# Moving the weight sums of two seven-product down projections to an earlier stage and another engine

## Chip, core and metric

The kernel runs on one core of a Trainium2 chip. The metric is the device time of one execution in microseconds, the median of several runs.

## What is computed

Two transformer blocks in sequence on one sequence of 1024 tokens with 1024 features, all in float32. What the change touches are both feed-forward networks, the first block's gated unit and its attention:

```python
# first block
xn = rms_norm(x, mix_norm_g)
q, k, v, f_logit, z = split(xn @ w_in)
attn = forgetting_attention(q, k, v, log_sigmoid(f_logit + b_f))   # 8 heads, causal
sgu  = spatial_gating(gelu(z), ...)
x = x + concat(rms_norm(attn), rms_norm(sgu)) @ w_out
gate, up = split(rms_norm(x) @ w_gate_up)
x = rms_norm(x + (silu(gate) * up) @ w_down, final)                 # w_down: 2816 x 1024
# second block: convolutions, a delta rule in chunks, stick-breaking attention, w_mix_out
u = causal_dwconv(rms_norm(x) @ w_ffn_up); gate, val = split(u)
x = x + (silu(gate) * val) @ w_ffn_down                             # w_ffn_down: 2816 x 1024
```

## The kernel before

**Products.** A float32 matrix product is done as three passes of a reduced type: each operand is cut into a high part (a cast on ScalarE, `split`, L256) and a low part (a subtraction on VectorE, L257), and `mm3` issues high x high, high x low and low x high. The order of the instructions on each engine is made by a scheduler at build time from priorities that follow the program's order; at run time every engine works through its own list in order and waits on semaphores. A tile is followed by the regions that are read and written.

**Stages of block 1.** `zphase` projects `z` in four column blocks (b = 0 to 3, eight token tiles t each) and does the gated unit. `attention` then takes four pairs of heads p = 0 to 3: `gemm(p + 1)` makes q, k and v of the next pair while `attend(p)` does the scores, the exponentials, the transposes and the products with v of this one. The output of pair p goes to `OT[:, p, :]` (16 KB per partition in all): ScalarE copies one half of the sum out of PSUM (L657) and VectorE adds the other (L658). The bank `O` that it comes from has one buffer. The pool engine (GpSimd) has two memsets (`ql`, L527) between the start-up and the loads of `x` behind the attention (L743).

**Down projection.** `ffn` computes the hidden values in units and spills them to memory (`hd`). Then `strassen` multiplies the first 20 of 22 blocks of 128 hidden features as a 2 x 2 partition with seven products (`DOWN`, in the order A11 B11, A12 B21, S3 T3, A22 T4, S1 T1, S2 T2, S4 B22), each of ND = 10 steps k; a step is four token tiles of three passes, 12 matmuls of 128 x 512. A are the hidden values, B the weights (quarters of 1280 x 512, 2.6 MB each), S and T their sums:

S3 = A11 - A21, S1 = A21 + A22, S2 = A22 - S3, S4 = A12 - S2; T3 = B22 - B12, T1 = B12 - B11, T2 = B22 - T1, T4 = B21 - T2.

- *The A side.* `operand(i)` makes the sums for step i and cuts A or S into a slot of a ring `ah`; it runs AR = 3 steps ahead of the matmuls. `DE` says which engine does which sum. A22 comes through two slots `a22`, loaded step by step (`load22`, L1218).
- *The B side.* The pool `W` (class `Weights`) gives each weight piece a slot: a load through a ring of two raw buffers on the SP queue, a cut into one of three high/low buffers, in a fixed order. `add_down` makes the slots of the down projection, one for two steps k. B11, B12 and B21 lie whole in SBUF, loaded by `fetch` at the start of the stage (with A11, A12 and A21); B22 comes through the ring, once for T3 and once for its own product. When the slot of T3 is cut, VectorE makes T3 and T1, and the pool engine T2; when that of T4 is cut, the pool engine makes T4 (L845).

The matmuls' sums in PSUM are added into `x` by VectorE at L980 (`add`), two per step (`PB`), after a product has ended.

Of the kernel before, what the change touches and what calls it, by code (L numbers as in the profile page):

```python
# [40 lines left out]
ND, AR, A2, PB = 10, 3, 2, 2  # L41
# [11 lines left out]
DE = dict(S3=pool_, T3=vec_, T1=vec_, T2=pool_, T4=pool_, S1=vec_, S2=vec_, S4=pool_)  # L53
# [104 lines left out]
class Kern:  # L158
# [6 lines left out]
    def setup(self):  # L165
        tc, nc = self.tc, self.nc
        self.const = c = tc.alloc_tile_pool(name="const", bufs=1)
        self.xnp = tc.alloc_tile_pool(name="xn", bufs=1)
        self.W = Weights(self, tc.alloc_tile_pool(name="w", bufs=1), 2, 3)
        self.dram = tc.alloc_tile_pool(name="dram", bufs=1, space=DRAM)  # L170
        self.hd = self.dram.tile([NF, P, S], F32, name="hd")
        self.ident = c.tile([P, P], F32, name="ident")
        make_identity(nc, self.ident)
        self.eps = c.tile([P, 1], F32, name="eps")
        nc.vector.memset(self.eps, EPS)
# [175 lines left out]
    def block1(self):  # L351
# [22 lines left out]
        self.zphase(mid, zb, zu, fl)  # L374
# [6 lines left out]
    def zphase(self, mid, zb, zu, fl):  # L381
# [80 lines left out]
        zl = z2.tile([P, NT, 512], F32R, name="zl")  # L462
        for t in range(NT):
            zmm(1, t)
            st = z2.tile([P, 6], F32, tag="bst", name="bst", bufs=2)
# [3 lines left out]
        for t in range(NT):  # L469
            zmm(2, t)  # L470
            y = z2.tile([P, 512], F32, tag="lny", name="lny", bufs=2)
# [5 lines left out]
        for t in range(NT):  # L477
            zmm(3, t)

# [12 lines left out]
        pool.release()  # L492

# [25 lines left out]
    def attention(self, mid, qkv, zu, cT, fl, OT, wo):  # L519
# [6 lines left out]
        for x in range(2):  # L526
            nc.gpsimd.memset(ql[x][64 * (1 - x):64 * (2 - x)].bitcast(F32), 0.0)  # L527
# [288 lines left out]
    def plan_ffn(self, which):  # L816
# [13 lines left out]
        for _, name in DOWN:  # L830
            if which == 1 and name == "T2":
                rest()
            for k in range(0, ND, 2):
                slots[name, k] = self.add_down(home, name, k, dn)
# [4 lines left out]
    def add_down(self, home, name, k, dn):  # L839

        W, nc = self.W, self.nc
        raw = W.load([(0, dn[:, ND + k:ND + k + 2, 512:])], 2, 512) if name in ("T3", "B22") else None

        def tt(out, in0, in1, what):
            DE[what](nc).tensor_tensor(out=out, in0=in0, in1=in1, op=ALU.subtract)  # L845

        def make(hi, lo):
            out = []
            for j in range(2):
                h, l = (v[:, j * 512:(j + 1) * 512] for v in (hi, lo))  # L850
                b11, b12, b21 = (home.get((q, k + j)) for q in ("B11", "B12", "B21"))
                b22 = None if raw is None else W.raw[raw][:, j * 512:(j + 1) * 512]
                if name == "T3":
                    src = home["T3", j]
                    tt(src, b22, b12, "T3")
                    tt(b12, b12, b11, "T1")
                    tt(b11, b22, b12, "T2")
                else:
                    src = dict(B11=b11, B21=b21, T4=b21, T1=b12, T2=b11, B22=b22)[name]
                    if name == "T4":  # L860
                        tt(b21, b21, b11, "T4")
                self.split(h, l, src)
                out.append((h, l))
            return out
        return W.slot(make, raw)
# [76 lines left out]
    def ffn(self, which):  # L942
# [193 lines left out]
        def fetch(q, k0, k1):  # L1136

            f = k0 + ND * ((q[2] if q[0] == "A" else q[1]) == "2")
            c = 512 * ((q[1] if q[0] == "A" else q[2]) == "2")
            src = self.hd[f:f + k1 - k0, :, c:c + 512].rearrange("k p c -> p k c") if q[0] == "A" else \  # L1140
                dn[:, f:f + k1 - k0, c:c + 512]
# [9 lines left out]
        def down_load():  # L1151

            for q, part in (("A11", "hi0"), ("B11", "lo0")):
                place(q, self.xnp.tile([P, KT, 512], F32, tag=part, name=q), 0, KT)
            for k in range(0, KT, 2):
                fetch("A11", k, k + 2)
                fetch("B11", k, k + 2)
# [3 lines left out]
        def down_open():  # L1161
# [4 lines left out]
            ring["ah"] = [d.tile([P, 2, 512], F32R, name=f"ah{i}") for i in range(AR)]  # L1166
            d = tc.alloc_tile_pool(name=f"dm{which}", bufs=1, reuse_waits="tile")
            dp.append(d)
            for j in range(2):
                home["T3", j] = d.tile([P, 512], F32, name=f"T3{j}")  # L1170
            ring["a22"] = [d.tile([P, 512], F32, name=f"a22{i}") for i in range(A2)]
            for q in ("A11", "B11", "A21", "B12"):
                place(q, d.tile([P, ND - KT, 512], F32, name=f"{q}x"), KT, ND)
            for q, part in (("A21", "hi1"), ("B12", "lo1")):
                place(q, self.xnp.tile([P, KT, 512], F32, tag=part, name=q), 0, KT)
            fetch("A11", KT, ND)
            fetch("B11", KT, ND)
            fetch("A12", 0, ND // 2)
            fetch("A12", ND // 2, ND)
            for i in range(AR):  # L1180
# [39 lines left out]
        def load_rest():  # L1220

            dp.pop().release()
# [8 lines left out]
        def strassen():  # L1231
            pool.release()
            last = None
            d2 = tc.alloc_tile_pool(name=f"dr{which}", bufs=1, side="right", reuse_waits="tile")
            dp.append(d2)
            self.psum(dn=(1, 8))
            place("B21", d2.tile([P, ND, 512], F32, name="B21"), 0, ND)
            for q in ("B21", "A21", "B12"):
                cuts = ((0, ND // 2), (ND // 2, ND)) if q == "B21" else ((0, KT // 2), (KT // 2, KT), (KT, ND))
                for k0, k1 in cuts:  # L1240
                    fetch(q, k0, k1)
            for k in range(A2):
                load22(k)
            sums = []
            for i, (name, bname, k) in enumerate(steps):
# [14 lines left out]
                w = W.get(slots[bname, k - k % 2])[k % 2]  # L1260
# [20 lines left out]
            if which == 1:  # L1281
                W.done(slots[DOWN[-1][1], ND - 2])
            return last
# [13 lines left out]
        else:  # L1297
# [3 lines left out]
            dp[1].release()  # L1301
# [956 lines left out]
```

## Time and profile before

| | |
|---|---|
| median of 3 runs (lowest to highest) | 2526.09 us (2524.6 to 2533.17) |
| the profiled execution: time, span | 2535.99 us, 2534.3 us |
| TensorE busy, granted clock | 2425.8 us (96%), 0.984 |
| VectorE, ScalarE, GpSimd busy | 1849.4, 1148.9, 431.7 us |
| first block's `z` projections; attention | about 17 to 118 us; 118 to 425 us |
| down projections in seven products | from 949 us and from 2288 us |

The span runs from the first to the last instruction. Engine names in the profile: PE is TensorE (PEld its weight loads), DVE VectorE, ACT ScalarE, POOL GpSimd, SP the queue from which most transfers are issued. A granted clock of 1.00 is the upper of TensorE's two levels (2.4 GHz), a mean below it says that part of the time was spent at the lower one (1.2 GHz).

### The profile page before, as it was taken

How to read it: one execution, taken by the hardware profiler on the slowest of the kernel's cores; microseconds unless marked ns; L12 is line 12 of the kernel's file. 1: busy time of each engine (PE TensorE's matmuls, PEld its weight loads, DVE VectorE, ACT ScalarE, POOL GpSimd, SP SyncE). 2: the span in 40 equal slices, each digit the busy share in tenths (PEclk: the TensorE clock that was granted, in tenths of full speed). 3: DMA queues.
4: the chain of work that ended last, by engine and by line, in shares of the span. 5: the costliest groups of instructions: out<-in, count | busy, mean ns of one | idle time of the engine just before them, and what ended most of it. 6: DMA issues, size and time to landing. Idle time of an engine off the chain costs nothing. (4 is left out here: it accounts for less than half of the span.)

```text
span 2534.3 us, 33313 instructions
## 1 busy us (share of the span) xinstructions
PE 2425.8 (96%) x12360; PEld 1997.5 (79%) x12360; DVE 1849.4 (73%) x3346; ACT 1148.9 (45%) x2298; POOL 431.7 (17%) x402
## 2 busy tenths in 40 slices
PE   7999999999999999899999999989889999999898
PEld 7977779978888887588877777879678888887677
DVE  5557788655555558977667768777878788878977
ACT  5356676342322233337533344776744434434243
POOL 1000002031111114500200000232341111113600
PEclk9999999999999999999998999999999999999999
DMA  4110002112222236213211112141212222227112
GB/s 152 51 34 24 19 26 92 42 50 76 75 85 90 75 115 234 75 42 120 72 35 34 46 43 67 35 143 49 75 51 84 92 75 75 83 92 265 67 34 109
DMA packets 194675, 196.58 MB, mean 78 GB/s; under 512 B 11613, under 2 KB 154032, under 8 KB 194512
## 3 DMA queue, kind: packets, MB, share of 16 engines
q1 hardware_dynamic: 189760, 178.74, 21.9%
q0 software_dynamic: 4752, 15.71, 1.7%
q8 instruction: 97, 1.59, 0.3%
q14 instruction: 66, 0.54, 0.1%
HBM read 155.76 MB, written 38.67 MB: 77 GB/s over the span
## 5 line engine op out<-in xcount | busy, mean ns | idle before, releaser
L257 DVE TENSOR_TENSOR wl<-wr,wh 128x512 fp32r<-128x512 f32 (+4 forms) x388 | 300.9, 804 | 320.8 <-ACT wh L256 316.7
L256 ACT CAST wh<-wr 128x512 fp32r<-128x512 f32 (+4 forms) x388 | 257.3, 696 | 594.0 <-PE st L973 364.2
L269 PE MATMUL dn<-wh,ah 128*128 128x512 f32 x560 | 226.6, 405 | 21.6 <-DVE ah L257 21.4
L267 PE MATMUL dn<-wh,ah 128*128 128x512 f32 x560 | 226.3, 404 | 6.7 <-ACT ah L256 3.4
L268 PE MATMUL dn<-wl,ah 128*128 128x512 f32 x560 | 223.8, 400 | 0.0
L980 DVE TENSOR_TENSOR u<-st,u 128x512 f32<-128x512 f32 x260 | 168.0, 685 | 31.1 <-PE st L973 29.8
L878 POOL TENSOR_TENSOR wr<-wr 128x512 f32<-128x512 f32 x42 | 55.3, 1316 | 692.0 <-DVE wr L878 692.0
L269 PEld LDWEIGHTS dn<-wh,ah 128*128 128x128 f32 x560 | 107.4, 192 | 56.4 <-DVE ah L257 31.1
L973 PE MATMUL st<-f2hi,wl 128*128 128x512 f32 x368 | 147.0, 400 | 0.0
L973 PE MATMUL st<-f2lo,wh 128*128 128x512 f32 x368 | 147.0, 399 | 0.0
L973 PE MATMUL st<-f1hi,wl 128*128 128x512 f32 x368 | 146.9, 399 | 0.0
L973 PE MATMUL st<-f1lo,wh 128*128 128x512 f32 x368 | 146.4, 398 | 0.0
L973 PE MATMUL st<-f2hi,wh 128*128 128x512 f32 x368 | 145.0, 394 | 0.7 <-ACT f2hi L256 0.7
L973 PE MATMUL st<-f1hi,wh 128*128 128x512 f32 x368 | 144.9, 394 | 0.7 <-ACT f1hi L256 0.7
L267 PEld LDWEIGHTS dn<-wh,ah 128*128 128x128 f32 x560 | 107.8, 193 | 33.8 <-ACT ah L256 5.1
L268 PEld LDWEIGHTS dn<-wl,ah 128*128 128x128 f32 x560 | 108.0, 193 | 24.3
L257 DVE TENSOR_TENSOR ah<-A,ah 128x512 fp32r<-128x512 f32 x104 | 83.9, 809 | 44.1 <-ACT ah L256 41.2
L256 ACT CAST ah<-A 128x512 fp32r<-128x512 f32 x104 | 63.7, 619 | 114.7 <-PE dn L268 98.9
L973 PEld LDWEIGHTS st<-f2hi,wh 128*128 128x128 f32 x368 | 70.4, 191 | 17.2 <-ACT f2hi L256 0.9
L973 PEld LDWEIGHTS st<-f1hi,wh 128*128 128x128 f32 x368 | 70.2, 191 | 17.0 <-ACT f1hi L256 0.9
L973 PEld LDWEIGHTS st<-f2lo,wh 128*128 128x128 f32 x368 | 69.6, 189 | 15.9
L973 PEld LDWEIGHTS st<-f1lo,wh 128*128 128x128 f32 x368 | 69.4, 189 | 16.1
(546 smaller groups left out, 7063.4 us busy)
## 6 DMA issues: line engine op xcount, KB each, us to landing
wr<-in_w_gate_up_dram SPq DMA_DIRECT2D x44, 512.0 KB, 4.2
hd<-sg SPq DMA_DIRECT2D x44, 512.0 KB, 3.1
wr<-in_w_ffn_up_dram SPq DMA_DIRECT2D x44, 512.0 KB, 3.8
wr<-in_w_mix_in_dram SPq DMA_DIRECT2D x28, 512.0 KB, 3.9
wr<-in_w_in_dram SPq DMA_DIRECT2D x16, 512.0 KB, 3.9
wr<-in_w_down_dram SPq DMA_DIRECT2D x12, 512.0 KB, 3.2
wr<-in_w_ffn_down_dram SPq DMA_DIRECT2D x12, 512.0 KB, 3.2
A<-hd SPq DMA_DIRECT2D x4, 1280.0 KB, 13.8
```

The lines of the kernel that those rows point to most:

```text
L256: self.nc.scalar.copy(hi, src)
L257: self.nc.vector.tensor_tensor(out=lo, in0=src, in1=hi.bitcast(F32), op=ALU.subtract)
L267: mm(out, a[0], b[0], start=start, stop=False)
L268: mm(out, a[0], b[1], start=False, stop=False)
L269: mm(out, a[1], b[0], start=False, stop=stop)
L878: SE[what](nc).tensor_tensor(out=raw(name), in0=raw(in0), in1=raw(in1), op=op)
L973: mm(ps, a[p][:, kk, :], b[q][:, kk, :], start=start and kk == 0 and j == 0, stop=kk == n - 1 and j == 2, skip_group_check=True)
L980: nc.vector.tensor_tensor(out=out, in0=ps, in1=t, op=ALU.add)
```

## The change

The sums T1 to T4 of both down projections are made once, ahead of time, by the pool engine, and written to memory (`td`). The generator `prepare_down` loads, for each of 10 blocks k of either projection, the four weight pieces (128 x 512, 256 KB) into parts of `OT`, makes T3, T1, T2 and T4 in place and stores each; loads and stores go through the pool engine's own queue. The first projection uses all eight parts of `OT`, the second the six of p = 1 to 3. The first eight loads each stand behind a one-column copy from `zv[:, 4]`. The generator is advanced behind every second token tile of b = 1, 2 and 3 in `zphase`, and run to its end ahead of `attention`, so that all of it stands in the pool engine's list before anything of the attention. The `ql` memsets go to VectorE.

In the down projection every B or T piece is then an ordinary slot of `W`, 128 x 1024, loaded raw through the ring (a B from the weights, a T from `td`). The whole tiles of B11, B12 and B21 and their fetches are gone. `ah` gets three more slots once the units' memory is free (AR = 6). S2 goes from VectorE to the pool engine; S3 and S4 were there already, S1 stays on VectorE.

```diff
-ND, AR, A2, PB = 10, 3, 2, 2
+ND, AR, AR0, A2, PB = 10, 6, 3, 2, 2
-DE = dict(S3=pool_, T3=vec_, T1=vec_, T2=pool_, T4=pool_, S1=vec_, S2=vec_, S4=pool_)
+DE = dict(S3=pool_, S1=vec_, S2=pool_, S4=pool_)
...
+        self.td = {(w, n): self.dram.tile([P, ND, 512], F32, name=f"td{w}{n}")
+                   for w in (1, 2) for n in ("T1", "T2", "T3", "T4")}
...
-        self.zphase(mid, zb, zu, fl)
+        prep = self.zphase(mid, zb, zu, fl, OT)
+        run_all(prep)
...
+        prep = self.prepare_down([OT[:, p, c:c + 512] for p in range(4) for c in (0, 512)], zv[:, 4, 0:1])
         for t in range(NT):
             zmm(1, t)
+            if t % 2:
+                next(prep)
...
-            nc.gpsimd.memset(ql[x][64 * (1 - x):64 * (2 - x)].bitcast(F32), 0.0)
+            nc.vector.memset(ql[x][64 * (1 - x):64 * (2 - x)].bitcast(F32), 0.0)
...
-    def add_down(self, home, name, k, dn):
...
+    def add_down(self, which, name, k, dn):
+        f, c = k + ND * (name[1] == "2"), 512 * (name[2:] == "2")
+        return self.W.add([(0, dn[:, f:f + 2, c:c + 512] if name[0] == "B" else self.td[which, name][:, k:k + 2, :])],
+                          2, 512)
+
+    def prepare_down(self, room, first):
+        nc = self.nc
+        blocks = [(which, k) for which in (1, 2) for k in range(ND)]
+        n, loaded = [0, 0], {}
+
+        def load(which, k):
+            dn = self.ffn_plan[which][3]
+            loaded[which, k] = []
+            for name in ("B12", "B22", "B11", "B21"):
+                f, c = k + ND * (name[1] == "2"), 512 * (name[2] == "2")
+                places = room[2 * which - 2:]
+                t = places[n[which - 1] % len(places)]
+                n[which - 1] += 1
+                if k < 2 and which == 1:
+                    nc.gpsimd.tensor_copy(t[:, 0:1], first)
+                nc.gpsimd.dma_start(out=t, in_=dn[:, f, c:c + 512])
+                loaded[which, k].append(t)
+
+        def keep(which, k, name, out, in0, in1, op):
+            nc.gpsimd.tensor_tensor(out=out, in0=in0, in1=in1, op=op)
+            nc.gpsimd.dma_start(out=self.td[which, name][:, k, :], in_=out)
+
+        load(*blocks[0])
+        yield
+        for i, x in enumerate(blocks):
+            b12, b22, b11, b21 = loaded.pop(x)
+            keep(*x, "T3", b22, b22, b12, ALU.subtract)
+            keep(*x, "T1", b12, b12, b11, ALU.subtract)
+            keep(*x, "T2", b11, b11, b22, ALU.add)
+            if i + 1 < len(blocks):
+                load(*blocks[i + 1])
+            keep(*x, "T4", b21, b21, b11, ALU.subtract)
+            yield
...
-            for q in ("A11", "B11", "A21", "B12"):
+            for q in ("A11", "A21"):
                 place(q, d.tile([P, ND - KT, 512], F32, name=f"{q}x"), KT, ND)
...
+            ring["ah"] += [d.tile([P, 2, 512], F32R, name=f"ah{i}") for i in range(AR0, AR)]
...
-                w = W.get(slots[bname, k - k % 2])[k % 2]
+                w = [v[:, k % 2, :] for v in W.get(slots[bname, k - k % 2])]
```

## Rows read from the trace of the kernel before

**Rows 1.** The head of the page and its part 1: the span, and of each engine the busy time, its share and its instructions.
```profile
span 2534.3 us, 33313 instructions
...
PE 2425.8 (96%) x12360; PEld 1997.5 (79%) x12360; DVE 1849.4 (73%) x3346; ACT 1148.9 (45%) x2298; POOL 431.7 (17%) x402
```
**Rows 2.** Busy time by stretch: the beginning and the middle of the first and of the second down projection, and the rest of the second. Columns: from and to, length, then busy time (and matmuls or instructions) of PE, PEld, DVE, ACT and POOL, granted clock, share of the transfer engines, GB/s.
```profile
949.00:1000.00 51.00, 50.41 (x216) 39.96 (x215) 40.82 (x58) 22.73 (x40) 17.42 (x11) 1.00 0.79 291
1000.00:1090.00 90.00, 76.30 (x292) 57.91 (x292) 87.47 (x108) 28.18 (x49) 52.13 (x31) 0.92 0.22 76
...
2288.00:2340.00 52.00, 50.30 (x218) 40.38 (x217) 44.13 (x64) 23.97 (x43) 19.36 (x12) 1.00 0.76 281
2340.00:2430.00 90.00, 77.77 (x305) 59.23 (x304) 87.82 (x109) 31.18 (x54) 50.15 (x29) 0.94 0.19 65
2430.00:2505.00 75.00, 75.00 (x325) 60.69 (x324) 47.88 (x75) 28.53 (x49) 0.60 (x1) 1.00 0.13 42
```
**Rows 3.** Waits in 1000 to 1090 us: who waited for whom, in all, times, longest.
```profile
PEld dn L269 <- DVE ah L257: 14.9, 10, 3.3
...
PE dn L269 <- DVE ah L257: 10.8, 8, 2.9
```
**Rows 4.** DVE's groups of instructions in 1000 to 1090 us: line, operation, out and in, shapes and count, then busy time and mean ns.
```profile
L257 DVE TENSOR_TENSOR ah<-A,ah 128x512 fp32r<-128x512 f32 x13 | 13.5, 1042 | 0.0
...
L845 DVE TENSOR_TENSOR T<-wr,B 128x512 f32<-128x512 f32 x6 | 7.0, 1187 | 2.2 <-DMA wr<-in_w_down_dram 2.2
...
L1194 DVE TENSOR_TENSOR A<-a,A 128x512 f32<-128x512 f32 x8 | 6.5, 817 | 0.0
L845 DVE TENSOR_TENSOR B<-B,B 128x512 f32<-128x512 f32 x6 | 5.2, 860 | 0.0
...
L845 DVE TENSOR_TENSOR B12x<-B12x,B11x 128x512 f32<-128x512 f32 x2 | 2.4, 1219 | 0.0
```
**Rows 5.** The same of POOL.
```profile
L845 POOL TENSOR_TENSOR B<-wr,B 128x512 f32<-128x512 f32 x7 | 15.8, 2257 | 4.4 <-DVE B L845 2.5 <-ACT ah L256 1.9
L845 POOL TENSOR_TENSOR B<-B,B 128x512 f32<-128x512 f32 x8 | 13.9, 1738 | 0.6
```
**Rows 6.** The timeline of DVE in the first down projection: start, duration, line, operation.
```profile
1015.41 1.75 DVE L257 TENSOR_TENSOR ah<-A,ah 128x512 fp32r<-128x512 f32 x1
1017.09 0.68 DVE L845 TENSOR_TENSOR B<-B,B 128x512 f32<-128x512 f32 x1
```
**Rows 7.** The timeline of POOL at the same place.
```profile
1015.02 1.59 POOL L845 TENSOR_TENSOR B<-B,B 128x512 f32<-128x512 f32 x1
```
**Rows 8.** DVE's additions out of PSUM in the down projections: count, shortest, median and longest duration in ns, first and last start.
```profile
L980 DVE TENSOR_TENSOR x<-dn,x x112: 671/679/692, 979.2 to 2504.9; 128x512 f32<-128x512 f32 x112
```
**Rows 9.** A step of the chain that ended last, at the start of the second down projection: start, duration, what.
```profile
2281.16 7.57 DMA B<-in_w_ffn_down_dram
```
**Rows 10.** The loads of `a22` by the SP queue.
```profile
DMA to landing us min/median/max: 2.5/2.6/11.9
```
**Rows 11.** Groups of POOL's instructions over the whole run: sums of two SBUF tiles, and the issue of a store of 256 KB.
```profile
L878 POOL TENSOR_TENSOR wr<-wr 128x512 f32<-128x512 f32 x42 | 55.3, 1316 | 692.0 <-DVE wr L878 692.0
...
L926 POOL TENSOR_TENSOR xs<-xs 128x512 f32<-128x512 f32 x24 | 36.8, 1541 | 75.8 <-DVE xs L926 66.3 <-PE xT L921 6.4 <-DVE rs L299 2.4
...
L1870 POOL DMA_DIRECT2D sqd<-sqt x8 | 4.4, 555 | 125.6 <-ACT sqt L1869 125.6
```
**Rows 12.** The timeline of POOL behind the attention: eight issues of loads, then three sums of 128 x 1024.
```profile
422.46 4.22 POOL L743 DMA_DIRECT2D x<-in_x_dram  x8 [329.04 <-PE O L653]
...
427.22 8.27 POOL L755 TENSOR_TENSOR sq<-sq,sq 128x1024 f32<-128x1024 f32 x3
```
**Rows 13.** Transfers of 256 KB issued by POOL and read back by SP (`sqd`): from issue to landing.
```profile
DMA to landing us min/median/max: 2.4/3.1/6.1
```
**Rows 14.** The timeline of ACT in `zphase`: the copy of `zv[:, 4]` in b = 0 and its activation in b = 1.
```profile
37.38 0.37 ACT L422 COPY zv<-z 128x256 f32<-128x256 f32 x1 [1.78 <-PE z L269]
...
63.19 0.41 ACT L241 ACTIVATE zv<-zv 128x256 f32<-128x256 f32 x1
```
**Rows 15.** The timeline of ACT in the attention: the first write of `OT[:, 0]` and the first of `OT[:, 1]`.
```profile
176.32 0.37 ACT L657 COPY OT<-O 64x256 f32<-64x256 f32 x1
...
238.48 0.37 ACT L657 COPY OT<-O 64x256 f32<-64x256 f32 x1
```
**Rows 16.** The timeline of PE: the first product into the next `O` after that write.
```profile
240.94 0.37 PE L649 MATMUL O<-PTh,V 128*128 128x256 f32 x1
```
**Rows 17.** Busy time by stretch: the end of `zphase`, the first projections of the attention, its first pair. Columns as in rows 2.
```profile
100.00:118.00 18.00, 18.00 (x150) 17.91 (x149) 0.70 (x1) 3.75 (x9) 0.00 (x0) 1.00 0.04 12
118.00:163.00 45.00, 45.00 (x204) 36.46 (x203) 19.64 (x26) 20.17 (x42) 0.00 (x0) 1.00 0.22 59
163.00:225.00 62.00, 60.29 (x343) 46.87 (x343) 49.70 (x159) 39.85 (x101) 0.00 (x0) 1.00 0.07 18
```
**Rows 18.** DVE's groups in 42 to 260 us.
```profile
L617 DVE TENSOR_SCALAR P<-P,small 128x512 f32<-128x512 f32 x18 | 8.6, 484 | 0.2
...
L617 DVE TENSOR_SCALAR P<-P,small 128x384 f32<-128x384 f32 x6 | 2.5, 416 | 0.0
...
L617 DVE TENSOR_SCALAR P<-P,small 128x256 f32<-128x256 f32 x7 | 2.5, 350 | 0.1
...
L617 DVE TENSOR_SCALAR P<-P,small 128x128 f32<-128x128 f32 x7 | 2.0, 285 | 0.0
```

## What is expected

> **What bounds the kernel now.** I read the head of the page first: TensorE is busy 96% of the span, so whatever can be won lies in the stretches where it is not [rows 1]. The busy time by stretch finds them. Undisturbed, the second down projection ends at 325 matmuls in 75 us, 0.231 us each; 90 us would hold 390. The middle of the first holds 292 in 90 us, that of the second 305 [rows 2]. Missing are 98 and 85 matmuls, 22.5 and 19.5 us, together 42 us (with the lower granted clock, 0.92 and 0.94, that goes with the gaps). In both stretches DVE is busy 87.5 and 87.8 of 90 us, ACT a third, POOL 50 to 52 us [rows 2]. The waits say the same: the matmuls and weight loads of `dn` wait for DVE's `ah` [rows 3]. So DVE bounds these two stretches, with POOL in its way: where a sum of POOL runs, a sum of DVE takes 1.75 us in the place of 0.68 [rows 6, 7], 1.07 us more, while DVE's additions out of PSUM stay at 671 to 692 ns throughout [rows 8].
>
> **What comes off the down projections.** From DVE's list in such a stretch go T3 and T1 (7.0 + 5.2 + 2.4 us) and S2 (6.5 us) [rows 4], 21 us of 87.5, which leaves 66. From POOL's go T2 and T4 (15.8 + 13.9 us) [rows 5], and ten S2 come, at 1.5 us each by the nearest rows [rows 11] 15 us: 37 us in the place of 52, so fewer sums of DVE are lengthened; the 13 `ah` cuts alone carry 13 x (1.04 - 0.68) = 4.7 us of that [rows 4]. DVE's demand is then some 62 us for the 292 matmuls, which at full rate take 292 x 0.231 = 67.5 us. It fits, at 92%. That is tight for single steps, and for those there is the ring: six steps of 12 matmuls are 16.6 us of cover where three were 8.3. I take 35 of the 42 us; bounds: 20 (a queue used at 92% gives half of it back) and 43 (all of it, and the edges of the stretches).
>
> What comes on there. The B side is loaded through the ring, 7 x 2.6 MB in place of 3 + 2 such quarters, but spread over some 195 us instead of piled up at the start. That pile shows once: a B fetch of 7.57 us stands in the chain at the start of the second projection [rows 9]; loaded through the ring, it is issued ahead of the A fetches. The beginning of the second has 218 matmuls in 52 us [rows 2], where 225 would go: worth 1.5 us, between 0 and 3. The two slots of `a22` are now freed by POOL's S2, not DVE's: load 2.6 us [rows 10], cut 1.3 us (ACT 0.6, DVE 0.7), S2 1.5 us, some 5.4 us for one slot or 2.7 us a step with two, against 2.8 us that PE takes for one. Nothing, while the ring is full; behind a late transfer it would be the next to stall.
>
> **What comes onto POOL.** Each of 20 blocks k has four sums, four loads and four stores. A sum of two 128 x 512 tiles takes POOL 1.32 us where DVE does little of the kind and 1.54 us beside DVE's sums [rows 11]; I take 1.45. An issue takes 0.53 to 0.56 us, eight of them 4.22 us without a gap, and the next sum starts at once [rows 11, 12]. So 4 x 1.45 + 8 x 0.555 = 10.2 us, and waits. In the second projection's blocks the load of B11 takes the place of T1 just stored; from the start of T1's store to that load POOL has T2, two issues of stores and two of loads, 3.7 us, and a 256 KB transfer lands after 3.1 us, up to 6.1 [rows 13]. T3 of the next block likewise has about 3.7 us from the issue of its B22. These waits lie between 0 and 2.3 us a block; I take 0.8, so 11.0 us a block (9.9 to 12.5).
>
> The start is set by the copy of `zv[:, 4]`, done at 37.75 us [rows 14]; two copies and issues (1.3 us) and a transfer (3.1 us [rows 13]) later, at 42 us, the first sum can start. The last block begins at 42 + 19b, where b is the time of a block; its T1 is stored after two sums and one issue (3.5 us) and landed 3.4 us later: 48.9 + 19b, or 258 us at b = 11.0. In return, the copies in front of the second four loads are done by about 51 us, 12 us ahead of the activation of `zv[:, 4]` that must wait for them [rows 14]: nothing.
>
> **Who waits for POOL.** T1 of that last block lies in `OT[:, 1]`, columns 0 to 511. The attention first writes there at 238.48 us (`OT[:, 0]`, at 176.32 us, was used last by the ninth block, done by 42 + 9 x 11 = 141 us) [rows 15]. So ACT would stand at that write, everything behind it on ACT with it (casts, exponentials), and PE from its next product into the single `O` bank, 2.5 us later [rows 16]. This stage is itself later by what follows, 5 us, so ACT waits 258 - 243.5 = 14.5 us, and PE loses 12. The write to `OT[:, 2]` comes some 67 us later, when POOL has ended.
>
> **What POOL does to DVE.** POOL's sums hold 5.8 of every 11 us, 53%. In `zphase` that meets the chain from L472 to the cut of `zh`, eight tiles of four instructions, at most 32 x 0.53 x 1.07 = 18 us; DVE is idle for 17.3 of the 18 us behind them [rows 17], so I set 0. In the first pair of the attention DVE is busy 49.7 of 62 us and PE already at 60.3 [rows 17]. Its operands are mostly in PSUM, which rows 8 show untouched. Uncovered is the scaling `P<-P`, 38 instructions [rows 18], of which no row stands beside a sum of POOL: 0 if it is like the PSUM form, and at most 38 x 0.53 x 1.07 = 21 us of DVE's time over the stretch to 260 us if it is like the two-tile form. DVE has 12 us of idle time to give in the first pair. I take 5 us of PE's time, between 0 and 12. The Trainium skill (SBUF — State Buffer, section Who interferes with whom) has it that DVE and GpSimd exclude each other for a whole instruction where DVE reads two SBUF tiles, and also where a `tensor_scalar` runs in a two-port mode. The trace agrees on the first (1.75 us beside 0.68), and no row shows the second; without the second the sum would be some 4 us lower, with it it stands.
>
> The `ql` memsets, on DVE, are two instructions of about 1 us in a stretch of 45 us with 19.6 us of DVE work [rows 17]: 0. POOL's transfers add 2.1 MB in 11 us, 190 GB/s, to 59 GB/s and less [rows 17]; 281 and 291 GB/s went through the first 50 us of the down projections, with 216 matmuls in 51 us [rows 2]. Behind the sums POOL next has the loads of `x`, at 422 us [rows 12]; nothing is queued between.
>
> **Sum.** -35 - 1.5 + 5 + 12 = -19.5 us. The sum is made against the profiled execution, 2535.99 us, which lies 9.9 us above the median of the runs; taken off the median, 2526.09, it gives 2507 us.
>
> **Rivals.**
>
> *POOL is in time* (chance 0.27). At b = 10.2 or less T1 lands by 243 us and nobody waits: -36.5 + 5, 2495 us. For it: the bare sum of instructions is just 10.2. Against it: no wait at all in 160 transfers.
>
> *The down projections stay bound by DVE and POOL* (0.13). 92% is an average; with S1, S2 and the cuts of A22 in one place the demand there is over 100%, and if six steps of cover don't carry it, 15 us come back: -16.5 + 17, 2527 us, no change.
>
> *POOL is late by much* (0.13), slower. Each 0.1 us of a block moves the end by 1.9 us. PE's loss equals the rest of the sum (-31.5) when ACT waits 34 us, at b = 12.0. At 12.5, with sums at 1.74 us as in the down projections [rows 5] and waits of 1.1 us, ACT waits 43 us, and the sum is +9: 2535 us.
>
> *The first write of `OT` waits for all sums* (0.07), if the order of the lists or the regions' bookkeeping ties it to the end: 265 us instead of 176, some 85 us for PE, -36.5 + 5 + 85: 2580 us.
>
> The forecast itself (0.40) has a range of its own of 2496 to 2518 us.
>
> **How the numbers follow.** Under 0.3% (7.6 us) this kernel's measurement can't tell from no change. Faster: forecast and POOL in time, with a little of the bound case, 0.70. Same: most of the bound case and a share of the late one, 0.12. Slower: the rest of the late case, the last, and the edge of the bound one, 0.18. For 8 in 10 the range reaches from a full gain of 43 us with small losses (2486) to the late case (2536).
>
> **What would show it.** In the middle of the down projections about 370 matmuls or more in 90 us and DVE under 80 us; POOL's block at 10.2 to 12 us, its last store near 262 us; one wait of ACT at L657's successor near 243 us for POOL or for a store of T1, and PE idle with it; `P<-P` longer than 0.48 us before that and not after. Wrong I am if b is off by 1 us (19 us of the end), if the waits at `OT` are spread out by other work of ACT placed ahead of the write, or if DVE isn't what a down step waits for once T3 and T1 are gone.

## The result, and the profile after

| | before | after |
|---|---|---|
| median of four runs, us | 2525.95 | 2552.16 |
| lowest to highest, us | 2524.6 to 2533.17 | 2549.13 to 2555.43 |
| profiled execution (its span), us | 2535.99 (2534.3) | 2552.18 (2550.5) |

The ratio is 1.0093, with an interval from 1.0073 to 1.0112: slower by 26 us, where a gain of 19 us was forecast. The profiled execution of after stands at the median of its runs; that of before stood 10 us above it, and a second profile of before, taken later, took 2523.09 us. Both are used below.

What the change does can be read off four marks. First the beginnings and middles of the two down projections of after, cut as in [rows 2] (same columns), from 0.6 and 0.2 us ahead of their first product.

```profile
996.40:1047.40 51.00, 48.95 (x208) 38.11 (x207) 42.09 (x48) 21.43 (x31) 17.20 (x10) 1.00 0.68 246
1047.40:1137.40 90.00, 87.89 (x379) 70.77 (x378) 75.07 (x80) 35.18 (x49) 35.64 (x21) 1.00 0.41 129
2314.00:2366.00 52.00, 48.15 (x194) 37.84 (x193) 46.56 (x54) 23.54 (x33) 18.32 (x10) 0.93 0.66 238
2366.00:2456.00 90.00, 87.39 (x371) 70.44 (x370) 74.68 (x78) 34.36 (x47) 33.85 (x20) 0.98 0.38 117
```

The middles hold 379 and 371 matmuls where they held 292 and 305: the gain that was forecast is there. The beginnings hold 208 and 194 where they held 216 and 218: there is a loss that was not. Next the stretches of [rows 17], the end of the first projection's products, the projections of the attention and its first pair.

```profile
100.00:118.00 18.00, 0.00 (x0) 0.00 (x0) 17.93 (x17) 2.77 (x6) 17.92 (x24) 0.53 0.64 221
118.00:163.00 45.00, 40.00 (x250) 36.20 (x251) 21.88 (x20) 15.53 (x36) 39.73 (x51) 0.92 0.74 243
163.00:225.00 62.00, 55.38 (x255) 43.47 (x254) 44.49 (x80) 28.87 (x61) 50.21 (x66) 0.92 0.67 221
```

For 18 us TensorE does nothing at all, in a stretch where it had been full, and VectorE, which had been idle there for 17.3 of 18 us, is busy throughout with 17 instructions. The waits of TensorE from 90 to 130 us name it (who waited for whom, us in total, times, longest):

```profile
PE z L270 <- ACT wh L259: 22.1, 1, 22.1
```

The groups of VectorE from 42 to 260 us show by how much its instructions grew (busy us, mean ns): five rows of before (`P<-P` is in [rows 18]), then six of after. Those of POOL over the whole run show what stood beside them.

```profile
L257 DVE TENSOR_TENSOR wl<-wr,wh 128x1024 fp32r<-128x1024 f32 x11 | 13.5, 1224 | 35.9 <-ACT wh L256 35.8
L257 DVE TENSOR_TENSOR zl<-lny,zh 128x512 fp32r<-128x512 f32 x8 | 5.5, 687 | 0.1
L474 DVE TENSOR_TENSOR lny<-lny,lg 128x512 f32<-128x512 f32 x8 | 5.4, 684 | 0.0
L475 DVE TENSOR_TENSOR lny<-lny,lb 128x512 f32<-128x512 f32 x8 | 5.5, 688 | 0.1
L472 DVE TENSOR_SCALAR lny<-zv,mv,rs 128x512 f32<-128x512 f32 x8 | 4.2, 543 | 0.1
```

```profile
L260 DVE TENSOR_TENSOR wl<-wr,wh 128x1024 fp32r<-128x1024 f32 x9 | 19.4, 2150 | 27.0 <-ACT wh L259 27.0
L260 DVE TENSOR_TENSOR zl<-lny,zh 128x512 fp32r<-128x512 f32 x8 | 14.0, 1752 | 0.1
L483 DVE TENSOR_TENSOR lny<-lny,lg 128x512 f32<-128x512 f32 x8 | 11.4, 1430 | 0.0
L484 DVE TENSOR_TENSOR lny<-lny,lb 128x512 f32<-128x512 f32 x8 | 11.3, 1413 | 0.1
L481 DVE TENSOR_SCALAR lny<-zv,mv,rs 128x512 f32<-128x512 f32 x8 | 10.4, 1320 | 0.1
L629 DVE TENSOR_SCALAR P<-P,small 128x512 f32<-128x512 f32 x10 | 9.4, 942 | 0.2
```

```profile
L879 POOL TENSOR_TENSOR OT<-OT 128x512 f32<-128x512 f32 x80 | 104.5, 1315 | 12.3 <-DMA OT<-in_w_down_dram 7.7 <-DMA OT<-in_w_ffn_down_dram 3.7
L880 POOL DMA_DIRECT2D td1T<-OT x40 | 22.4, 559 | 0.0
```

The chain of `zh`, eight tiles (`zl` and the three groups of `lny`), takes 47 us where it took 21, and `P<-P` 942 ns where it took 484 [rows 18]; the cuts of weights, `wl`, are lengthened too. POOL's sums take 1315 ns, as in the first of [rows 11]. Where a sum of POOL and such an instruction meet, nearly the whole wait falls on VectorE. These means mix two kinds: counted one by one in the trace, 18 of the chain's 32 instructions are lengthened, by 0.94 to 3.09 us, 1.48 in the mean, and the other 14 keep their length.

Why TensorE starves is seen in the two in-order queues, in the timelines of VectorE and ScalarE (start, duration). The first three rows show two lengthened instructions of the chain and one that isn't.

```profile
111.26 2.45 DVE L483 TENSOR_TENSOR lny<-lny,lg 128x512 f32<-128x512 f32 x1
113.63 1.48 DVE L481 TENSOR_SCALAR lny<-zv,mv,rs 128x512 f32<-128x512 f32 x1
115.03 0.68 DVE L484 TENSOR_TENSOR lny<-lny,lb 128x512 f32<-128x512 f32 x1
115.63 2.10 DVE L483 TENSOR_TENSOR lny<-lny,lg 128x512 f32<-128x512 f32 x1
117.66 0.15 DVE L431 TENSOR_TENSOR fl<-z,bf 128x8 f32<-128x8 f32 x1
```

```profile
117.84 0.38 ACT L244 ACTIVATE zu<-z 128x252 f32<-128x252 f32 x1 [1.49 <-DVE fl L431]
118.12 1.05 ACT L259 CAST wh<-wr 128x1040 fp32r<-128x1040 f32 x1
```

TensorE had ended the third group at 97 us. The cut of the fourth group's weights stands on ScalarE behind an activation that waits for `fl`, and `fl`, an instruction of 0.15 us, stands on VectorE behind the lengthened chain. Of the 27 us by which the last `z` is later, 22.1 are this wait and 2.1 the next one, for the low part of that cut, `wl`.

In the attention, from 145 us to the first `st`, no single wait stands out. TensorE's waits there sum to 21.1 us, where they were 8.2 before; the three longest are these:

```profile
PE cb L276 <- DVE cT L528: 3.4, 1, 3.4
PE PT L642 <- DVE P L629: 3.1, 2, 1.6
PE O L661 <- DVE OT L670: 2.7, 4, 1.5
```

All of VectorE's instructions from 126 to 260 us are together 23.6 us longer than the same forms in no_sums (an experiment below). `P<-P` has 11.6 of these (9 of 21 lengthened), the cuts `wl` 5.9 (4 of 7), and instructions of the gate and of the row sums the rest. The granted clock is 0.92 from 118 to 225 us, where it was 1.00: some products ran at the lower level.

At `OT`, where 12 us were forecast, nobody waited: POOL's last store was issued at 253.34 us, and the first write of the second pair came at 286.30 us (238.48 before [rows 15]):

```profile
253.34 0.56 POOL L880 DMA_DIRECT2D td2T<-OT  x1 [0.30 <-POOL OT L879]
```

```profile
286.30 0.37 ACT L669 COPY OT<-O 64x256 f32<-64x256 f32 x1
```

Lengths of the stages in us, worked out from first and last starts of the products `z`, `st` (the units of an FFN), `dn` (the down projections) and `svab` (in block 2):

| | before | before, second profile | after | without preparation (below) |
|---|---|---|---|---|
| start to the last `z` | 117.3 | 117.7 | 144.8 | 118.7 |
| from there to the first `st` | 383.5 | 382.2 | 402.4 | 382.5 |
| units of the first FFN | 448.6 | 447.6 | 449.5 | 449.3 |
| first down projection to its products of the rest | 163.2 | 161.0 | 145.2 | 145.2 |
| from there to the first `svab` | 81.9 | 81.9 | 84.9 | 85.0 |
| block 2 to the second FFN | 644.9 | 636.2 | 638.1 | 637.6 |
| units of the second FFN | 448.5 | 448.6 | 449.0 | 449.8 |
| second down projection | 216.6 | 216.4 | 206.5 | 205.5 |

The loss is 27 us in the first row and 19 to 20 in the second; the gain is 16 and 10 us in the two projections, less 3 us behind the first.

### The profile page after: what moved, and what is told of

It is laid out like the page before. It is cut to its first block, busy times and chain, and to the rows that moved or that the text cites. A ratio compares the mean times of both kernels' runs of the same rounds, so it can differ in the third digit from the quotient of the medians.

```text
span 2550.5 us, 33547 instructions
## 1 busy us (share of the span) xinstructions
PE 2421.0 (95%) x12360; PEld 1996.9 (78%) x12360; DVE 1870.3 (73%) x3218; ACT 1143.0 (45%) x2228; POOL 585.6 (23%) x628
## 5 line engine op out<-in xcount | busy, mean ns | idle before, releaser
L260 DVE TENSOR_TENSOR wl<-wr,wh 128x512 fp32r<-128x512 f32 (+3 forms) x438 | 395.9, 928 | 335.4 <-ACT wh L259 331.1
L259 ACT CAST wh<-wr 128x512 fp32r<-128x512 f32 (+3 forms) x438 | 319.0, 756 | 664.9 <-PE st L1000 374.0
L270 PE MATMUL dn<-wh,ah 128*128 128x512 f32 x560 | 223.4, 399 | 2.7 <-ACT ah L259 2.1
L272 PE MATMUL dn<-wh,ah 128*128 128x512 f32 x560 | 222.7, 398 | 2.4 <-DVE ah L260 2.3
L1000 PE MATMUL st<-f1hi,wh 128*128 128x512 f32 x368 | 145.2, 395 | 0.7 <-ACT f1hi L259 0.7
L879 POOL TENSOR_TENSOR OT<-OT 128x512 f32<-128x512 f32 x80 | 104.5, 1315 | 12.3 <-DMA OT<-in_w_down_dram 7.7
L270 PE MATMUL z<-wh,x1hi 128*128 128x256 f32 (+1 forms) x256 | 74.7, 292 | 24.1 <-ACT wh L259 22.1
```

What stands on the lines that cost most here:

```text
L259: self.nc.scalar.copy(hi, src)
L260: self.nc.vector.tensor_tensor(out=lo, in0=src, in1=hi.bitcast(F32), op=ALU.subtract)
L270: mm(out, a[0], b[0], start=start, stop=False)
L272: mm(out, a[1], b[0], start=False, stop=stop)
L879: nc.gpsimd.tensor_tensor(out=out, in0=in0, in1=in1, op=op)
L1000: mm(ps, a[p][:, kk, :], b[q][:, kk, :], start=start and kk == 0 and j == 0, stop=kk == n - 1 and j == 2, skip_group_check=True)
```

## Experiments

**Theory A**: POOL's sums hold VectorE's instructions back, in the chain of `zh` and at `P<-P`. **B**: it is the transfers, 160 of 256 KB, 42 MB in all (the first expectation below counts twice that). **C**: it is the new order of instructions. **D**: it is POOL's issues.

### Sums, transfers or order

no_sums leaves out the sums alone, no_prep the whole preparation (T slots then load pieces of the weights as they are); prep_only adds it to the kernel before, and nothing reads it.

```diff
# no_sums
-            nc.gpsimd.tensor_tensor(out=out, in0=in0, in1=in1, op=op)
             nc.gpsimd.dma_start(out=self.td[which, name][:, k, :], in_=out)
# no_prep
-        prep = self.zphase(mid, zb, zu, fl, OT)
-        run_all(prep)
+        self.zphase(mid, zb, zu, fl, OT)
```

> The changed kernel without POOL's 80 sums: the pieces of the down weights are loaded by POOL's queue and stored again unsummed, so the down projections multiply with raw pieces; all loads, stores and slots stay. Theory A (POOL's sums hold VectorE's two-input instructions back, in the chain of zh and in the attention's first pair): the last z product ends near 120 us and not at 145, P<-P 128x512 back at 0.5 us, time 2505 to 2515 us. Theory B (the 40 MB of loads and 40 MB of stores delay the weights): no better than the changed kernel, 2545 to 2555. Theory D (POOL's issues of transfers hold VectorE back): between, 2530 to 2550.

> The changed kernel without the preparation: no loads, sums or stores on POOL before the attention's output; the slots of the down sums load raw pieces of the down weights, so their sums are left out of the computation. What stays is the gain side: no sums beside the down projections, six blocks of A ahead. Theories A, B and D: 2526 less the 32 us that the two down projections lost in the trace of the changed kernel, 2490 to 2500 us. Rival C (a different order of instructions, not POOL, costs the 46 us ahead of the first unit): above 2510, with the first st still near 547 us.

> The kernel before with the preparation added and its sums never read: the down projections sum their weights again as before. All theories but C: the cost alone, 2526 + 46 = 2565 to 2578 us. If cost and gain are not independent (the changed kernel's loss is partly in the down projections): under 2560.

Measured: no_sums 2504.52 us, ratio to before 0.9908 (0.9893 to 0.9924); no_prep 2504.27, 0.9909 (0.9889 to 0.9929); prep_only 2576.22, 1.0189 (1.0165 to 1.0214). no_sums ended 0.5 us below its range and no_prep 4 us above: it had taken 32 us off for the two projections, and 22 came. The two without sums agree to 0.3 us: transfers and issues cost nothing that can be measured, and the new order of the rest costs nothing ahead of the first FFN either. B, C and D fall. The sums cost 2552.2 - 2504.5 = 48 us in the changed kernel, and the whole preparation 50 us in the kernel before; the change without its price is worth 22 us. In no_sums VectorE's groups (42 to 260 us) are those of before, though the transfers, POOL's and those of the projections' weights, run at 226 to 287 GB/s beside them (100 to 225 us):

```profile
L484 DVE TENSOR_TENSOR lny<-lny,lb 128x512 f32<-128x512 f32 x8 | 5.5, 688 | 0.1
L481 DVE TENSOR_SCALAR lny<-zv,mv,rs 128x512 f32<-128x512 f32 x8 | 4.2, 543 | 0.1
L629 DVE TENSOR_SCALAR P<-P,small 128x512 f32<-128x512 f32 x18 | 8.7, 489 | 0.2
```

### What in a sum holds VectorE back

```diff
-            nc.gpsimd.tensor_tensor(out=out, in0=in0, in1=in1, op=op)
+            for c in (512, 512, 384):
+                nc.gpsimd.memset(out[:, :c], 0.0)
```

> The changed kernel with each POOL sum replaced by three memsets of the same tile (512, 512 and 384 columns), near 1.3 us together by the 0.95 us of a 1024-column memset, so that POOL writes as long but reads nothing; the T sums are zeros. Theory A in its narrow form (it is POOL's reads that hold back instructions with two SBUF inputs): zl<-lny and the two lny steps at 0.68 to 0.8 us, P<-P, which reads one tile, still near 1.0 us, time 2510 to 2530 us. Theory A in its wide form (any POOL instruction excludes them): zl<-lny still at 1.4 us and more, 2545 to 2555. Theory B: 2545 to 2555 with VectorE's instructions at their old length.

Measured: 2533.1 us, 1.0025 (1.0012 to 1.0038); its groups of VectorE from 42 to 260 us:

```profile
L629 DVE TENSOR_SCALAR P<-P,small 128x512 f32<-128x512 f32 x15 | 19.0, 1267 | 0.2
...
L481 DVE TENSOR_SCALAR lny<-zv,mv,rs 128x512 f32<-128x512 f32 x8 | 5.7, 728 | 0.1
L260 DVE TENSOR_TENSOR zl<-lny,zh 128x512 fp32r<-128x512 f32 x8 | 5.5, 684 | 0.1
L484 DVE TENSOR_TENSOR lny<-lny,lb 128x512 f32<-128x512 f32 x8 | 5.5, 683 | 0.1
```

The narrow form of A holds. Beside a POOL that only writes, the chain's instructions with two SBUF tiles keep their length, and the last `z` is at 119.1 us; the `tensor_scalar` forms are still held back, `P<-P` more than by the sums, and the way from there to the first `st` is 411 us in place of 382. Three memsets last 1.5 us, longer than a sum, and go on to some 290 us, so more of the attention is hit: that is probably the miss of 3 us above the expected range. The Trainium skill (SBUF — State Buffer, section Who interferes with whom) says both: an instruction of DVE with two SBUF inputs contends with GpSimd's reads and not with its writes, and one in a two-port mode with either. The rows agree: 1413 ns beside sums and 683 beside memsets for the first, 942 and 1267 beside 484 for the second.

### The two stages apart, and the queue

first_ten keeps the sums of the first ten blocks only. order and order2 try to take the weights' cut out from behind the chain: order by the text alone, order2 by a dependence.

```diff
# first_ten
-            nc.gpsimd.tensor_tensor(out=out, in0=in0, in1=in1, op=op)
+            if which == 1:
+                nc.gpsimd.tensor_tensor(out=out, in0=in0, in1=in1, op=op)
# order, order2: a loop of its own for the chain
         for t in range(NT):
             zmm(2, t)
+        last = self.cut.ins                       # order2
+        for t in range(NT):
             y = z2.tile([P, 512], F32, tag="lny", name="lny", bufs=2)
...
+            if t == 4:                            # order2
+                tc.add_manual_dep(ins.ins, last.name, NOSYNC, reason="order")
```

> The changed kernel with the sums of the second ten blocks left out (their pieces are loaded and stored raw, so the second down projection is computed from raw pieces); the first ten blocks, which run from 43 to 150 us, keep their sums. Theory A: the first projection's loss stays (last z product near 145 us), the attention's goes (P<-P 128x512 at 0.5 us in the mean of its first pair): 2552 less 19, 2530 to 2537 us. If the attention's loss came from the first projection's lateness or from the transfers: above 2545.

> The changed kernel with the first projection's third group of products written ahead of the chain of zh (tensor_scalar, lg, lb, cut) instead of woven with it tile by tile, so that fl and the cut of the fourth group's weights no longer stand behind the chain in the queues of VectorE and ScalarE; POOL's sums stay. Theory A with the queue as the way by which the chain reaches TensorE: TensorE's 22 us wait for wh is gone, the last z product ends near 120 us and not at 145, the sums that follow (sg) start when the slowed chain is through, near 126 us; time 2532 to 2540 us. Rival (the fourth group isn't held by the order, and TensorE only waits later): first sg still near 145 us, time 2548 to 2555.

> The changed kernel with the order forced: the chain of zh of tiles 4 to 7 may only start on VectorE behind the cut of the fourth group's weights (a dependence without a semaphore, so only the place in the queue changes); the text order alone had left the queues as they were. POOL's sums stay. Theory A with the queue as the way by which the chain reaches TensorE: the wait of 18.7 to 22 us for wh gone, last z product near 120 us, the sums behind it wait for the second half of the slowed chain (4 tiles of 5.9 us behind 100 us: near 126 us); 2532 to 2538 us. Rival (the slowed chain costs the same wherever it stands, because the products sg wait for all of it): 2546 to 2553 us.

Measured: first_ten 2531.27 us; order 2548.75; order2 2532.83 (1.0039, 1.0023 to 1.0054). In us:

| | last `z` | from there to the first `st` |
|---|---|---|
| after | 144.8 | 402.4 |
| first_ten | 143.6 | 383.8 |
| order | 141.4 | 403.6 |
| order2 | 123.3 | 405.9 |
| memsets | 119.1 | 411.0 |

first_ten has the whole first loss and nearly none of the second: they are two losses, each made by the sums that run beside that stage. order lies in its rival's range and decides nothing: the scheduler left the queues all but as they were (the text's order alone didn't move them), and the wait was still 18.7 us. order2 moved four tiles of the chain behind the cut. POOL's sums are all there, and the chain still takes 39 us in all:

```profile
PE z L270 <- ACT wh L259: 3.4, 1, 3.4
```

Against after that is 18.7 us less wait, and 19.3 us less time. The chain is 8 us shorter than in after, which can't make up 18.7 us of wait alone. So in the first stage it was not the chain itself that TensorE lacked, but the weights queued behind it.

### The gain: 22 us, where 36 were forecast

> The kernel before once more, for a second profile of it. The first profiled execution took 9.9 us more than the median of its runs. If that excess lay outside the down projections, this one is near 2526 us with the stretch from the first to the second FFN near 879 us, as in the kernel with the preparation added and unused, and not 890; the stretch of the first down projection up to its products of the rest near 160 us in both.

> The kernel without the preparation (raw pieces in place of the down sums), with three blocks of A ahead in place of six. If the sums taken off the down projections are the gain: within 6 us of its sister with six, 2504 to 2511 us. If the six blocks ahead are most of the gain of 22 us: 2515 us or more.

> The kernel without the preparation (raw pieces in place of the down sums), and POOL's two multiplications xs by gm (128x1024, 2.6 us) at the end of the first down projection moved to VectorE. In its sister's trace a cut of weights started beside one of them takes 2.95 us in place of 1.25, an addition out of PSUM is queued behind it, TensorE waits 2.1 us for that and then runs at the lower clock: the products svab start 85.0 us behind the first product of the rest, where the kernel before has 81.9. If that collision is the 3.1 us: svab near 82 to 83 us, time 2500.5 to 2503 us. If VectorE's longer list (two instructions of 1.3 us more) costs as much: no change, 2503 to 2506 us.

The last two are no_prep with one edit more:

```diff
# no_prep_three
-ND, AR, AR0, A2, PB = 10, 6, 3, 2, 2
+ND, AR, AR0, A2, PB = 10, 3, 3, 2, 2
# no_prep_tail
-TP = (6, 7)
+TP = ()
```

before_again, as expected (2523.09 us): of the first profile's excess, 8.7 us lie in block 2, which the change doesn't touch, and 2.2 us in the first down projection. The forecast's 42 us of missing matmuls were little affected: here the middles hold 299 and 306.

```profile
998.70:1088.70 90.00, 76.40 (x299) 57.95 (x298) 86.56 (x107) 29.22 (x52) 50.75 (x31) 0.94 0.23 76
...
2327.50:2417.50 90.00, 76.60 (x306) 58.50 (x305) 87.41 (x108) 31.05 (x54) 49.24 (x29) 0.96 0.20 65
```

no_prep_three: 2503.74 us, no different from six blocks ahead. In its trace three blocks cost 3.3 us in the first projection (148.3 us from its first product to its rest, in place of 145.0), but the way from there to `svab` is 81.9 us and not 85.0. The reason for that is another collision, in the trace of no_prep, of VectorE (first row) and POOL (second):

```profile
1172.12 2.95 DVE L260 TENSOR_TENSOR wl<-wr,wh 128x1056 fp32r<-128x1056 f32 x1 [0.17 <-ACT wh L259]
```

```profile
1169.20 4.76 POOL L314 TENSOR_TENSOR xs<-xs,gm 128x1024 f32<-128x1024 f32 x2 [37.62 <-ACT xs L244]
```

A cut of 1.25 us takes 2.95 beside POOL's multiplication, and an addition queued behind it lets TensorE wait for 2.1 us. In no_prep_tail, with that multiplication on VectorE, `svab` starts 81.4 us behind the first product of the rest; the time is 2501.56 us (0.9906, 0.9891 to 0.9921), in the expected range but its interval overlaps that of no_prep, so the 3 us are shown in place and not by the clock.

### Whether the preparation pays elsewhere

The rule that the runs above suggest is that a collision costs time where VectorE's queue sets TensorE's pace. ffn_prep, units and split put sums into the first FFN, where TensorE is full and VectorE half idle; split and which1 put the first ten blocks ahead of the attention, with a pause beside the chain of `zh`.

```diff
# ffn_prep, units (split: every second unit, blocks of the second projection only)
+            prep = self.prepare_down([pool.tile([P, 512], F32, name=f"pr{i}") for i in range(4)])
         for f in range(1, NF):
             unit(f)
+            next(prep, None)
# units, split: a block's loads stand behind the unit's own sums on POOL
+                self.tc.add_manual_dep(ins.ins, self.last_sum.name, NOSYNC, reason="pace")
# split, which1: the pause, in load()
+                if k in (3, 4):
+                    nc.gpsimd.tensor_copy(t[:, 0:1], zu[:, 0, 300:301])
# which1, made from the kernel before: its second projection sums as before
-                slots[name, k] = self.add_down(home, name, k, dn)
+                slots[name, k] = self.add_summed(name, k, dn) if which == 1 else self.add_down(home, name, k, dn)
```

> The changed kernel with the preparation moved: no loads, sums or stores of down weights ahead of the attention's output; instead POOL makes one block of sums per unit of the first FFN, in four tiles of its own of 512 columns, two units of 19.5 us short of all 22. There VectorE is 54 to 56 of 100 us busy and TensorE 100 of 100 in the trace of the kernel without the preparation. Theory A with the rule that a collision costs time only where VectorE's queue sets TensorE's pace: VectorE's two-input instructions beside a sum at 1.3 us and more, busy 65 to 75 of 100, TensorE still full; 2503 to 2512 us, faster than both kernels. Rival (the cuts of the units' weights come late as the cut of the projection's did): the units take 460 us and more in place of 449, 2516 to 2540 us.

> All 20 blocks of the preparation inside the first FFN, one per unit, with loads, sums and stores of a block placed in POOL's queue right behind the unit's own two weight sums, in four tiles of its own; nothing on POOL ahead of the attention's output. Unlike the earlier kernel with the sums in the FFN, no load overtakes a sum that still reads its tile, and POOL's own weight sums don't stand behind a wait. VectorE 55 to 56 of 100 us busy there without the sums, 4 sums of 1.3 us per unit of 19.5 us. Theory A with the rule that a collision costs time only where VectorE's queue sets TensorE's pace: 2502 to 2512 us, faster than both kernels. Rival (any collision in a stage that TensorE fills is passed on): 80 collisions of 0.6 to 1.0 us, 2550 to 2585 us.

> The ten blocks of the first down projection's weights on POOL ahead of the attention, but with a pause: behind the third block POOL waits for the fourth group's first activation (zu of tile 0, at 97.8 us in the trace before), so that no sum stands beside the chain of zh; seven blocks of 10.5 us follow, to about 171 us. The ten blocks of the second one's weights go into the first FFN, one in every second unit, right behind the unit's own weight sums. Theory A with the rule that a collision costs time only where VectorE's queue sets TensorE's pace: the last z product near 118 us, the attention no more than 3 us late, the units 449 to 454 us in place of 449, 2505 to 2513 us, faster than both kernels. Rival (with sums in the units the time wanders, as in the kernel with all twenty there): median 2518 to 2530 us with a spread over 20 us.

> Only the first down projection's ten blocks are prepared on POOL, with the pause beside the chain of zh; the second down projection sums its weights as the kernel before does, three blocks of A ahead in both. Sum from the runs: the stretch of the first down projection up to its rest 16 us shorter than before (160.8 to 145), 3 us back at its end, and the price of ten paused blocks ahead of the units, 5.7 us (first st 506.9 against 501.2): 2526 - 16 + 3 + 6, 2517 to 2521 us, faster than both kernels by little. If the price of the paused blocks is as large as that of unpaused ones (27 us): 2535 to 2542 us.

Measured: ffn_prep 2599.75 us; units 2526.57 (0.9999, 0.9973 to 1.0025), with runs from 2512 to 2554; split 2535.25 (1.0027, 1.0016 to 1.0037); which1 2517.89, **0.9966 (0.9954 to 0.9979)**. which1 is faster than both kernels, as expected; the three with sums in the FFN missed, their rivals' ranges too. In ffn_prep the loads of the next block stand ahead of T4 and go into the same four tiles, so its T4 are of other pieces; and by POOL's list its own weight sums stood behind the preparation, which waited for transfers, while TensorE waited (500 to 1000 us):

```profile
PE st L988 <- DVE u L995: 65.7, 9, 15.2
```

In units that is gone, and still the FFN isn't free, so the rule doesn't hold as it stands. Two windows of units and the same of no_prep:

```profile
600.00:700.00 100.00, 98.51 (x422) 78.97 (x422) 67.19 (x87) 28.72 (x51) 61.07 (x72) 1.00 0.56 184
```

```profile
600.00:700.00 100.00, 100.00 (x433) 81.31 (x432) 56.08 (x90) 29.95 (x53) 12.91 (x10) 1.00 0.27 79
```

422 matmuls in place of 433: 2.5% of 449 us, though VectorE is idle for a third of the time. The units take 457 us, and a wait of 7.2 us for `ah` follows at the start of the down projection. That profile is of the fastest of its runs (2512.3 us); what the slower ones lose beyond it was not seen. In split ten blocks cost more there than twenty in units (465 us for the units, 8.7 us at the down projection); why stays open. In which1 (three blocks of A ahead, S2 on POOL in the first projection) the pause keeps the chain of `zh` whole (last `z` at 118.1 us); the seven blocks behind it cost 5.4 us up to the first `st` (387.9 us in place of 382.5), and the first down projection takes 148.5 us in place of 161.0.

## Why the prediction was wrong

**What comes off the down projections: right.** 35 us were taken for the two middles. 379 - 292 and 371 - 305 are 153 matmuls at 0.231 us, 35 us (33 against the second profile). VectorE is down to 75 us of 90, as forecast (under 80). The cover of six steps that the forecast leaned on was worth 3 us, in the first projection, and was lost again behind it.

**What comes on there: wrong by 9 us.** The beginnings were to gain 1.5 us, the B side being spread out. They hold 8 and 24 matmuls less, 7 us. By the waits after, TensorE waits there for `wl` and `ah` of VectorE and ScalarE. It isn't the preparation: no_prep has 209 and 195 matmuls there. With three blocks ahead it is 207 and 212, so most of the second loss goes with the three added blocks (no_prep, then no_prep_three):

```profile
2268.10:2320.10 52.00, 48.35 (x195) 38.01 (x194) 46.98 (x54) 23.81 (x35) 18.49 (x10) 0.93 0.66 239
2268.50:2320.50 52.00, 49.67 (x212) 39.18 (x211) 47.37 (x55) 23.10 (x33) 17.22 (x10) 1.00 0.67 239
```

What makes the first one was not isolated. Another 3 us were in no term: the collision behind the first projection.

**POOL's block, and who waits for POOL: wrong by 12 us, and by luck.** The block took 10.5 us (sums of 1.31, not 1.45), so POOL was done near 253 us, and the attention itself came so late that its write at `OT` had 33 us to spare. The term of 12 us is nothing. But the T1 that the forecast had in mind was stored at 248.96 us and landed at 251.3: by these times a write at 243.5 us, where the forecast had it, would still have waited 8 us.

**What POOL does to VectorE: this is where the prediction failed.** For `zphase` the step was "DVE is idle for 17.3 of the 18 us behind them [rows 17], so I set 0"; 27 us were measured. It has two faults. The size: 18 us were worked out from 1.07 us a collision on 53% of 32 instructions, 17 of them. The number of collisions was right, 18; the price was not, 1.48 us and not 1.07, which came from a single pair of rows, and the chain grew by 26 us. And the cover, which weighs more: idle time behind the chain covers nothing for what is queued behind the chain and needed ahead of that idle time. TensorE's next weights were. order2 shows it: half of the chain in another place, 19 us.

In the attention 5 us were taken for `P<-P`, with 12 as the bound; the stage lost 20. `P<-P` is held back beside sums as the two-tile form is, as its upper case had it, but it is chance that 20 is near the 21 us worked out for that case: `P<-P` grew by 11.6 us, and about as much lies in instructions that the forecast left out, the cuts `wl` first of all. The idle time of VectorE that was to absorb this did not.

Together, by the profiles: -35 + 7 + 3 in and behind the projections, 20 in the attention, 27 in `zphase`, 22 us; the medians say 26. Of the rivals none came true: POOL was in time, as the first of them had it, and that decided nothing. The sum of the second is off: it counts the 5 us of `P<-P` twice, and -36.5 + 15 + 17 would be 2522 us, not 2527.

## What to carry to other kernels

Before work is put on POOL, look not at how idle POOL is but at which of VectorE's instructions beside it read two SBUF tiles or are `tensor_scalar` on one; take it that POOL's share of them collides (here 18 of 32, where POOL was adding for about half of the time), and count for each of these a whole POOL instruction and some more (here 1.48 us beside sums of 1.31). Then go through the in-order queues behind them for the next weights or tiles that TensorE needs: idle time that comes later is no cover for these. And take a second profile of the kernel before if the first stands above its median.

## What was not expected of the hardware

- The meeting of the two engines is one-sided here: 80 sums of POOL took 1315 ns in the mean, with an issue of 0.55 us behind each, while VectorE's instructions went from 684 and 687 to 1430 and 1752 ns. In the down projections POOL's sums were longer too [rows 5].
- A POOL that only writes (memsets of 0.43 to 0.54 us) leaves the chain's two-tile instructions at 681 to 684 ns and takes `P<-P` from 489 to 1267 ns, more than sums do (942).
- The preparation's transfers, 42 MB in 210 us beside the weights of the projections (226 to 287 GB/s in no_sums), cost TensorE nothing: 152, 207 and 344 matmuls in the stretches of [rows 17], 150, 204 and 343 before.
